# FFN in two phases over a DRAM copy of the gated features, and grid tokens laid out in blocks of 8 columns

## Chip, cores, metric

One core of a Trainium2 chip runs the whole program. The metric is the device time of one execution in microseconds (us), the median over the runs of a kernel. TensorE is called PE here, VectorE DVE, ScalarE ACT, GpSimd POOL; SyncE (SP) issues nearly all DMAs, and its queue is worked off in order.

## What is computed

Two layers with shared structure run over 128 context tokens and 1024 latent tokens (a grid of 16 rows by 64 columns). In each layer:

```
h = rms_norm(x) * (1 + sc_m) + sh_m
q, k, v of three head groups = split(h @ w_in)      # 6 neighbourhood heads, 4 MLA heads, 6 GQA heads
# neighbourhood head, latent token at (r, c): keys of 8 rows (clipped) x 16 columns (clipped) + 128 cached context keys,
#   col_start = clip(c - 8, 0, 48), row_start = clip(r - 4, 0, 8); bias rpb[row offset, column offset]
# MLA and GQA heads: all 1024 latent keys + 128 context keys
x = x + gt_m * rms_norm(concat(o_na, o_mla, o_gqa) @ w_out)
h = rms_norm(x) * (1 + sc_f) + sh_f
u = h @ w_up                                        # 1024 -> 2 x 2816
u = u[t-1] * conv_w[0] + u[t] * conv_w[1] + u[t+1] * conv_w[2] + conv_b     # along the tokens, t in row order of the grid
x = x + gt_f * rms_norm((silu(gate) * val) @ w_down)                        # 2816 -> 1024
```

## The kernel before

Tokens stand in 9 tiles of 128: tile 0 is the context, tiles 1 to 8 are the latent tokens, two grid rows each. Products are computed to float32 accuracy from pairs of float32r operands (a rounded part "hi" and a rest "lo"): hi*hi, hi*lo and lo*hi, so each product is three matmuls. `load_w` brings 128x1024 float32 weights into `wraw` (2 buffers), ACT casts them to "hi", and POOL or DVE subtracts to get "lo" (`split`). Instructions are put in order by a scheduler when the program is built; each engine then works off its own list in order.

A layer runs through these stages:

- **phase_a**: projections of h. The first product of layer 1 (values, weights `w0`) follows the FFN of layer 0 directly, and takes h tile by tile as the norm generators (`norm_tiles`, `h_group`) deliver it.
- **phase_b**: attention, head by head: 4 MLA and 6 GQA heads (`Task.dense`), then 6 neighbourhood heads (`Task.na`). A head is 8 tiles of 128 queries and one of context. A step scores one tile (`SA`), lets DVE add bias and mask and take the maximum (L829), ACT take the exponential, POOL normalise it (L708); three steps later PE transposes the probabilities (L719), ACT and DVE evacuate them as hi and lo (L200, L201), and PE multiplies by V (`pv_items`, L737). With two grid rows in a tile, the 8-row window of a query tile reaches over 4 tiles of keys in the tiles at the edge and 5 inside, plus the context tile: 640 or 768 columns. `load_bias` brings bias and mask as one `bint` tile and four `bedge` tiles, 17 pieces a head with their memsets.
- **phase_c**: output projection, norm, residual.
- **phase_d**: the FFN, in one loop over 22 features `f` of 128. For each it does the up products of the gate (`pg`, 3 PSUM banks of 384 tokens) and of the value (`pv_`, 3 banks): 72 matmuls each (L1025). `conv` gives ACT the centre tap and DVE the two shifted taps (`shifted`, L1037); ACT does SiLU; `gate` multiplies on POOL (L1059) and splits the result into `g`. Every second feature, `down` multiplies the two waiting `g` with their `w_down` rows for all 9 token tiles into `aux` (2 banks), 6 matmuls a bank (L1072), and DVE adds each bank into `Y` in SBUF (L1077). Beside it run the generators `extra` (`ada_dve`, L306): DVE's share of the modulation vectors, in layer 0 also those of layer 1.
- **The end of the FFN** (`last`): the last two features' products are done tile by tile; then `norm_tiles` reads `Y`, normalises, adds the residual, stores x, and in layer 0 makes h of layer 1. Tiles go in `PAIRS`.

## Time and profile before

| | |
|---|---|
| median of 3 runs | 3474.81 us (3470.6 to 3475.94) |
| the profiled execution | 3465.22 us |
| its span, first to last instruction | 3463.4 us |
| granted PE clock, mean | 0.982 of 2.4 GHz |
| busy: PE, DVE, ACT, POOL | 3266.7, 2263.4, 1486.0, 1073.9 us (94, 65, 43, 31%) |
| DMA | 339.33 MB, mean 98 GB/s |

The stages in us from the span's start: attention of layer 0 from about 365 to 758, its FFN from 889.0 to 1754.2, the values' product of layer 1 to 1832.7, attention of layer 1 from about 2060 to 2480, its FFN from 2602.9 to the end. PE is the engine to look at first: what counts is where it waits, and for whom, stage by stage, and not its share of the whole.

### The profile page before, as it was taken

How to read it: one execution, taken by the hardware profiler on the slowest of the kernel's cores; microseconds unless marked ns; L12 is line 12 of the kernel's file. 1: busy time of each engine (PE TensorE's matmuls, PEld its weight loads, DVE VectorE, ACT ScalarE, POOL GpSimd, SP SyncE). 2: the span in 40 equal slices, each digit the busy share in tenths (PEclk: the TensorE clock that was granted, in tenths of full speed). 3: DMA queues.
4: the chain of work that ended last, by engine and by line, in shares of the span. 5: the costliest groups of instructions: out<-in, count | busy, mean ns of one | idle time of the engine just before them, and what ended most of it. 6: DMA issues, size and time to landing. Idle time of an engine off the chain costs nothing. (4 is left out here: it accounts for less than half of the span.)

```text
span 3463.4 us, 50333 instructions
## 1 busy us (share of the span) xinstructions
PE 3266.7 (94%) x18380; PEld 2936.7 (85%) x18380; DVE 2263.4 (65%) x4955; ACT 1486.0 (43%) x3085; POOL 1073.9 (31%) x1062
## 2 busy tenths in 40 slices
PE   8989999999999999999988899999989999999996
PEld 4868888877889889899967799888779999999995
DVE  5796788886756755655497728888877433334437
ACT  4321788884422222222264228888753222222222
POOL 2121445541322222222242314455312223222223
PEclk9999999999999999999999899999999999999998
DMA  6467421453222222221144563115523111111113
GB/s 236 137 186 225 135 67 45 108 149 128 97 80 85 86 61 67 85 74 61 43 143 125 148 187 102 52 44 138 172 94 96 49 43 49 43 43 43 37 38 115
DMA packets 193415, 339.33 MB, mean 98 GB/s; under 512 B 18448, under 2 KB 107920, under 8 KB 193168
## 3 DMA queue, kind: packets, MB, share of 16 engines
q1 hardware_dynamic: 191872, 334.93, 32.4%
q8 instruction: 145, 2.38, 0.3%
q10 hardware_dynamic: 1296, 1.19, 0.1%
q14 instruction: 102, 0.84, 0.1%
HBM read 260.61 MB, written 75.43 MB: 97 GB/s over the span
## 5 line engine op out<-in xcount | busy, mean ns | idle before, releaser
L1025 PE MATMUL mm<-hhi,wu 128*128 128x384 f32 x4224 | 873.7, 336 | 2.4 <-POOL wu L195 1.5
L1025 PEld LDWEIGHTS mm<-hhi,wu 128*128 128x128 f32 x4224 | 746.8, 188 | 7.1 <-POOL wu L195 2.1
L1037 DVE SCALAR_TENSOR_TENSOR acc<-mm,conv,acc 128x127 f32<-128x127 f32 (+2 forms) x704 | 314.6, 509 | 335.3 <-ACT acc L1042 335.1
L1072 PE MATMUL aux<-wd,g 128*128 128x512 f32 x2160 | 501.5, 391 | 16.3 <-DVE Y L1077 11.3
L1025 PE MATMUL mm<-hlo,wu 128*128 128x384 f32 x2112 | 497.5, 335 | 0.0
L1072 PEld LDWEIGHTS aux<-wd,g 128*128 128x128 f32 x2160 | 405.3, 188 | 101.8 <-DVE Y L1077 13.4
L1025 PEld LDWEIGHTS mm<-hlo,wu 128*128 128x128 f32 x2112 | 379.4, 188 | 0.8 <-DVE hlo L151 0.4
L195 POOL TENSOR_TENSOR wu<-wraw,wu 128x1024 fp32r<-128x1024 f32 x90 | 218.8, 2433 | 466.5 <-ACT wu L192 433.7
L737 PE MATMUL O<-PT,V 128*128 128x256 f32 (+1 forms) x2080 | 349.3, 296 | 6.5 <-DVE Y L744 3.9
L1077 DVE TENSOR_TENSOR Y<-Y,aux 128x512 f32<-128x512 f32 x324 | 220.8, 686 | 182.3 <-PE aux L1072 181.9
L708 POOL TENSOR_SCALAR P<-P,rs 128x1152 f32<-128x1152 f32 (+3 forms) x288 | 291.2, 1012 | 151.3 <-DVE rs L707 120.7
L719 PE MATMUL T<-ident,P 128*128 128x128 f32 x1856 | 299.1, 277 | 16.5 <-DVE PT L201 11.5
L689 PE MATMUL SA<-k,q 128*128 128x512 f32 (+5 forms) x1224 | 301.0, 366 | 8.5 <-ACT ko L611 4.0
L195 POOL TENSOR_TENSOR wd<-wraw,wd 128x1024 fp32r<-128x1024 f32 x46 | 111.2, 2417 | 631.1 <-ACT wd L192 631.1
L201 DVE TENSOR_TENSOR PT<-T,PT 128x512 fp32r<-128x512 f32 (+1 forms) x448 | 290.2, 656 | 25.1 <-ACT PT L200 19.2
L737 PEld LDWEIGHTS O<-PT,V 128*128 128x128 f32 x2080 | 279.1, 190 | 21.5 <-DVE Y L744 10.0
L192 ACT CAST wd<-wraw 128x1024 fp32r<-128x1024 f32 x50 | 52.4, 1050 | 524.5 <-PE aux L1072 401.0
L200 ACT CAST PT<-T 128x512 fp32r<-128x512 f32 (+1 forms) x448 | 247.7, 568 | 57.2 <-PE T L719 44.2
L719 PEld LDWEIGHTS T<-ident,P 128*128 128x128 f32 x1856 | 213.9, 141 | 57.1 <-DVE PT L201 16.1
L306 DVE SCALAR_TENSOR_TENSOR aacc<-wadv,sc,aacc 128x512 f32<-128x512 f32 x280 | 218.7, 814 | 46.5 <-DMA wadv<-w_ada 45.5
L689 PEld LDWEIGHTS SA<-k,q 128*128 128x128 f32 (+1 forms) x1224 | 199.1, 192 | 33.6 <-ACT P L699 6.7
L192 ACT CAST wu<-wraw 128x1024 fp32r<-128x1024 f32 x94 | 98.7, 1052 | 260.4 <-PE mm L1025 260.1
(222 smaller groups left out, 5232.8 us busy)
## 6 DMA issues: line engine op xcount, KB each, us to landing
wraw<-w_up SPq DMA_DIRECT2D x88, 512.0 KB, 3.5
wadv<-w_ada SPq DMA_DIRECT2D x160, 256.0 KB, 2.7
wraw<-w_down SPq DMA_DIRECT2D x44, 512.0 KB, 3.5
k<-KT SPq DMA_DIRECT2D x64, 320.0 KB, 6.2
q<-QT SPq DMA_DIRECT2D x48, 288.0 KB, 5.2
XD<-xt SPq DMA_DIRECT2D x27, 512.0 KB, 2.6
xt<-XD SPq DMA_DIRECT2D x27, 512.0 KB, 4.2
wraw<-w_in SPq DMA_DIRECT2D x24, 512.0 KB, 3.7
```

The lines of the kernel that those rows point to most:

```text
L195: (lo_eng or pool).tensor_tensor(out=lo, in0=raw, in1=hi.bitcast(F32), op=ALU.subtract)
L200: act.copy(hi, src)
L201: dve.tensor_tensor(out=lo, in0=src, in1=hi.bitcast(F32), op=ALU.subtract)
L306: dve.scalar_tensor_tensor(out=accs[i], in0=w, scalar=sc[:, k, i:i + 1], in1=accs[i], op0=ALU.mult, op1=ALU.add)
L689: pe.matmul(out, q[0:rows, qc:qc + 128], kview(k[0:rows]), start=(i == 0), stop=(i == len(passes) - 1))
L708: pool.tensor_scalar(out=P[:, :n], in0=P[:, :n], scalar1=rs, scalar2=1.0, op0=ALU.mult, op1=ALU.mult)
L719: pe.transpose(tp[:, j * 128:(j + 1) * 128], p, ident)
L737: pe.matmul(op[0][:, :n], V[:, vt, :], PT[e][:, sl, :n], start=(i == 0 and e == 0), stop=(i == last and e == 1))
L1025: pe.matmul(pts[c][:, :CN], a[:, k, :], h_[:, k, c * CN:(c + 1) * CN], start=(k == 0 and a is whi and h_ is hhi), stop=(k == KC - 1 and a ...
L1037: dve.scalar_tensor_tensor(out=d, in0=pts[c][:, lo_ - c * CN:hi_ - c * CN], scalar=cw[:, wi:wi + 1], in1=d, op0=ALU.mult, op1=ALU.add)
L1072: pe.matmul(pt, g[:, ts], d[:, 0, js], start=(n == 0), stop=(n == tot - 1))
L1077: dve.tensor_tensor(out=Y[:, t, js], in0=Y[:, t, js], in1=pt, op=ALU.add)
```

## The change

Two things are changed, in both layers.

**Grid tokens by blocks of 8 columns.** The host reorders the latent tokens, so that a tile of 128 holds all 16 rows of 8 columns. The 16-column window of a query tile then reaches over 3 tiles of keys (2 at the two edges) and the context tile: 512 or 384 columns. The row window is done by the mask alone. One bias tile a head comes in one DMA (`b_na`). Probabilities of a tile go through one transposing step instead of one and a half; a pair of query tiles shares slots of `PT`, and keys that only one of them sees are multiplied by V in 128 columns. The convolution runs along grid rows, so neighbours at a block's edge now stand in another tile: `shifted` takes 7 of 8 columns inside the blocks and further small pieces for the edges, 8 instructions for each direction instead of 4.

**FFN in two phases.** `phase_u` does up products, convolution and gate for all 22 features and stores the gated values, unsplit, in DRAM (`GT`, 576 KB a feature). `Down` then goes over groups of three token tiles. A group keeps 6 PSUM banks open over all 22 features; for each it loads the `w_down` rows again (512 KB) and the group's slice of `GT` (192 KB), splits both, and does 18 matmuls. `Y`, its adds and the two-bank `aux` stage are gone. A tile is normalised from PSUM when its group is done (`tile_done`), the tiles of a group one after the other, with the last 2 features of a group (4 at the very end) done tile by tile. Splits of even steps put the weights' lo on POOL and the gated values' on DVE, odd steps the other way round. Loads run 3 features ahead. In the last layer each tile of y is stored in two halves.

```diff
+            b = bp.tile([128, 1280], F32, name="bias", bufs=2)
+            nc.sync.dma_start(out=b, in_=I["b_na"][l, h])
+            return [b[:, 512:896]] + [b[:, 0:512]] * 6 + [b[:, 896:1280]]
...
-            for i, (vt, sl) in enumerate(slots):
+            for i, (vt, sl, c0, c1) in enumerate(slots):
                 if not op:
                     op.append(bps.tile([128, 256], F32, name="O", bufs=1))
                 for e in range(2):
-                    pe.matmul(op[0][:, :n], V[:, vt, :], PT[e][:, sl, :n],
+                    pe.matmul(op[0][:, c0:c1], V[:, vt, :], PT[e][:, sl, c0:c1],
...
             def na(self, hd, pair, a):
                 i = 2 * pair + a
+                lo, hi = max(i - 1, 0), min(i + 2, 8)
+                n = self.n = (hi - lo + 1) * 128
                 qc = 128 + i * 128
+                k0 = 2 + lo
                 m = small("mx")
                 s = bank2()
                 self.P = new_p()
                 self.pieces, self.mneg, self.sign = [(self.P[:, :n], 0)], m[:, 0:1], -1.0
                 def sc_a():
+                    scores(s[:, 0:256], hd.passes, qc,
                            lambda k: k.rearrange("p (b n) -> p b n", n=128)[:, 1:k0 + 1:k0 - 1, :])
+                    scores(s[:, 256:n], hd.passes, qc,
+                           lambda k: k[:, (k0 + 1) * 128:(2 + hi) * 128])
+                    dve.tensor_tensor_reduce(out=self.P[:, :n], in0=s[:, 0:n],
                                              in1=hd.bias[i][:, :n], op0=ALU.add, op1=ALU.min, scale=-1.0,
                                              scalar=3.0e38, accum_out=m[:, 0:1])
                 self.sc = [sc_a]
+                own = [0, 2, 3, 1] if a == 0 and pair else list(range(hi - lo + 1))
                 qs = slice(a * 128, (a + 1) * 128)
+                def tr():
+                    if a == 0:
                         hd.PT[pair] = new_pt()
+                    transpose_p([self.block(b) for b in own],
+                                [o[:, 0:len(own), qs] for o in hd.PT[pair]])
+                self.tr = [tr]
+                b0 = 2 + 2 * pair
+                slots = [(1, 0, 0, 256)]
+                if pair > 0:
+                    slots.append((b0 - 1, 3, 0, 128))
+                if pair < 3:
+                    slots.append((b0 + 2, 3, 128, 256))
+                slots += [(b0, 1, 0, 256), (b0 + 1, 2, 0, 256)]
+                self.pv = (lambda: pv_items(hd.V, hd.PT[pair], slots, 256, hd.hg,
+                                            128 + pair * 256)) if a == 1 else None
                 return self
...
+            fr = slice(0, 7) if sh == 1 else slice(1, 8)
+            to = slice(1, 8) if sh == 1 else slice(0, 7)
+            fe, te = (7, 0) if sh == 1 else (0, 7)
+            b0, nb, o = (0, 2, 128) if c == 0 else (3 * c - 1, 3, 0)
+            if c == 0:
+                f0 = 0 if sh == 1 else 1
+                add(acc[:, f0 + sh:f0 + sh + 127], pts[0][:, f0:f0 + 127])
+            src = pts[c][:, o:o + nb * 128].rearrange("p (g i) -> p g i", i=8)
+            dst = acc[:, 128:NT].rearrange("p (g i) -> p g i", i=8)
+            add(dst[:, b0 * 16:(b0 + nb) * 16, to], src[:, :, fr])
+            if sh == 1:
+                n = min(nb, 7 - b0) * 16
+                add(dst[:, (b0 + 1) * 16:(b0 + 1) * 16 + n, te], src[:, 0:n, fe])
+                if n < nb * 16:
+                    add(dst[:, 1:16, te], src[:, n:n + 15, fe])
+            else:
+                k = 1 if b0 == 0 else 0
+                add(dst[:, (b0 + k - 1) * 16:(b0 + nb - 1) * 16, te], src[:, k * 16:nb * 16, fe])
+                if k:
+                    add(dst[:, 112:127, te], src[:, 1:16, fe])
...
+        def gate(ag, av):
+            pool.tensor_tensor(out=av, in0=ag, in1=av, op=ALU.mult)
+            nc.sync.dma_start(out=GT[l][f], in_=av)
+
+        def along():
+            for _ in range(3):
+                advance(extra)
...
             else:
                 up_mm(wg, pg, range(NCH))
+            ag = conv(pg, f, 0)
+            act.activation(out=ag, in_=ag, func=AF.Silu)
+            along()
+            if f > 0:
                 wv = load_up(f + NFF)
                 pv_ = [mm() for _ in range(NCH)]
                 up_mm(wv, pv_, range(NCH))
+            av = conv(pv_, f + NFF, 1)
+            gate(ag, av)
+            along()
...
+    DOWN = ((0, 1, 2), (3, 4, 5), (6, 7, 8))
+    AHEAD = 3
+    class Down:
+        def __init__(self, l, wp, gp):
+            self.l, self.wp, self.gp = l, wp, gp
+            self.seq = [(g, f) for g in range(len(DOWN)) for f in range(NFF)]
+            self.parts = {}
+        def load(self, i):
+            if i >= len(self.seq) or i in self.parts:
+                return
+            g, f = self.seq[i]
+            e, o = (dve, pool) if i % 2 else (pool, dve)
+            wd = load_w(self.wp, I["w_down"][self.l, f], ("wd", "wu")[i // 2 % 2], 2, e)
+            n = 128 * len(DOWN[g])
+            raw = self.gp.tile([128, CN], F32, name="graw", bufs=2)[:, :n]
+            nc.sync.dma_start(out=raw, in_=GT[self.l][f][:, DOWN[g][0] * 128:DOWN[g][0] * 128 + n])
+            gs = [self.gp.tile([128, CN], F32R, name=f"g{j}", bufs=4)[:, :n] for j in range(2)]
+            split(raw, *gs, lo_eng=o)
+            self.parts[i] = gs, wd
+        def products(self, i, t, pts, js):
+            g, f = self.seq[i]
+            (ghi, glo), (dhi, dlo) = self.parts[i]
+            ts = slice((t - DOWN[g][0]) * 128, (t - DOWN[g][0] + 1) * 128)
+            for n, (a, d) in enumerate(((ghi, dhi), (ghi, dlo), (glo, dhi))):
+                for j in js:
+                    pe.matmul(pts[j], a[:, ts], d[:, 0, j * 512:(j + 1) * 512], start=(f == 0 and n == 0),
+                              stop=(f == NFF - 1 and n == 2))
+        def run(self, tile_done, step, before_tail, tail_last):
+            for g, tiles in enumerate(DOWN):
+                end = g == len(DOWN) - 1
+                tail = tail_last if end else 2
+                pts = {t: [mm(), mm()] for t in tiles}
+                i0 = g * NFF
+                for f in range(NFF - tail):
+                    self.load(i0 + f + AHEAD)
+                    for t in tiles:
+                        self.products(i0 + f, t, pts[t], (0, 1))
+                    step()
+                for f in range(NFF - tail, NFF):
+                    self.load(i0 + f)
+                self.load(i0 + NFF)
+                if end:
+                    before_tail()
+                for t in tiles:
+                    for j in (0, 1):
+                        for f in range(NFF - tail, NFF):
+                            self.products(i0 + f, t, pts[t], (j,))
+                    tile_done(t, pts[t])
+                self.load(i0 + NFF + 1)
+                self.load(i0 + NFF + 2)
...
+        def tile_done(t, banks):
+            xt = load_x(ep, XD[2 * l], t, "xt", 4)
+            wt = ep.tile([128, D], F32, name="wt", bufs=4)
+            A, B = (zn.Am, zn.mods[:, 0]) if zn is not None else (None, None)
+            gens.append(norm_tiles(ep, (t,), [banks], [junk], [wt], [xt], G, xo, A, B, H, xs, GROUPS, (dve, dve)))
...
+        down.run(tile_done, lambda: advance(gens), lambda: more_w0((0, 1)), 4 if zn is None else 2)
+        more_w0((2, 3))
```

What an engine works off, and in which order, is decided when the program is built. Three places matter for what follows; the numbers behind names are buffers.

The first is SP's list in the middle of the FFN of layer 1. Before, loads of the up weights (`w_up`, two a feature) and of the down weights (`w_down`, one a feature) follow each other:

```order
L343 DMA wraw_32215<-w_down 128x1024
L343 DMA wraw_32221<-w_up 128x1024
L343 DMA wraw_32459<-w_up 128x1024
L343 DMA wraw_32557<-w_down 128x1024
L343 DMA wraw_32563<-w_up 128x1024
L343 DMA wraw_32657<-w_up 128x1024
L343 DMA wraw_32755<-w_down 128x1024
```

In the change the stores of the gated values stand among the loads of the up weights. Here `GT16` and `GT17` are features 6 and 7 of layer 1, and the loads ahead of each store are those of the feature two further on (8 ahead of the store of 6, 9 ahead of 7):

```order
L348 DMA wraw_29603<-w_up 128x1024
L348 DMA wraw_29705<-w_up 128x1024
L1054 DMA GT16_116<-acc1_29376 128x1152
L348 DMA wraw_29808<-w_up 128x1024
L348 DMA wraw_29910<-w_up 128x1024
L1054 DMA GT17_117<-acc1_29581 128x1152
L348 DMA wraw_30013<-w_up 128x1024
L348 DMA wraw_30115<-w_up 128x1024
```

The down weights' loads have left this stretch, and a store, which waits for POOL's product of its feature, has none of the next feature's loads behind it.

The second is SP's list in the down phase, a stretch that did not exist before (the loads of `w_down` then stood among those of `w_up`, as above). This is group 0 of layer 0, features 12 to 15, the slice of gated values (`graw`) and the weights (`wraw`) of each:

```order
L1109 DMA graw_15984<-GT012_100 128x384
L348 DMA wraw_15978<-w_down 128x1024
L1109 DMA graw_16014<-GT013_101 128x384
L348 DMA wraw_16008<-w_down 128x1024
L1109 DMA graw_16044<-GT014_102 128x384
L348 DMA wraw_16038<-w_down 128x1024
L1109 DMA graw_16074<-GT015_103 128x384
L348 DMA wraw_16068<-w_down 128x1024
```

Before, a load of `w_down` stood between every two of `w_up`; now each feature of each group has two loads, alternately, and each waits for the split that frees its buffer two features back: `wraw` for POOL's in even features and for DVE's in odd ones, `graw` the other way round.

The third is PE's list in the last neighbourhood head of layer 0 (`k0`, `k1` are hi and lo of the keys, `SA` scores, `T` transposed probabilities, `O` the product with V). Before, two inner tiles:

```order
L689 MATMUL SA_9449<-k0_9130,q0_9138 128x256
L689 MATMUL SA_9449<-k1_9133,q0_9138 128x256
L689 MATMUL SA_9449<-k0_9130,q0_9138 128x512
L689 MATMUL SA_9449<-k1_9133,q0_9138 128x512
L719 MATMUL T_9464<-ident_63,P_9354 128x128 x4
L737 MATMUL O_9471<-PT1_9400,V_8818 128x256
L737 MATMUL O_9471<-PT0_9399,V_8818 128x256
L737 MATMUL O_9471<-PT1_9400,V_8818 128x256
L689 MATMUL SA_9486<-k0_9130,q0_9138 128x256
L689 MATMUL SA_9486<-k1_9133,q0_9138 128x256
L689 MATMUL SA_9486<-k0_9130,q0_9138 128x512
L689 MATMUL SA_9486<-k1_9133,q0_9138 128x512
```

Now, an inner tile and the product of an inner pair:

```order
L679 MATMUL SA_8662<-k0_8394,q0_8402 128x256
L679 MATMUL SA_8662<-k1_8397,q0_8402 128x256
L679 MATMUL SA_8662<-k0_8394,q0_8402 128x256
L727 MATMUL O_8618<-PT0_8553,V_8146 128x256
L679 MATMUL SA_8662<-k1_8397,q0_8402 128x256
L727 MATMUL O_8618<-PT1_8554,V_8146 128x256
L727 MATMUL O_8618<-PT0_8553,V_8146 128x128
L727 MATMUL O_8618<-PT1_8554,V_8146 128x128
L727 MATMUL O_8618<-PT0_8553,V_8146 128x128
L727 MATMUL O_8618<-PT1_8554,V_8146 128x128
L727 MATMUL O_8618<-PT0_8553,V_8146 128x256
L727 MATMUL O_8618<-PT1_8554,V_8146 128x256
```

The second score piece went from 512 to 256 columns, the transposes of a tile from five or six to four, and the product of an inner pair from 14 matmuls of 256 columns to 10, of which four have 128.

## Rows read from the trace of the kernel before

**Rows 1.** Windows by stage: length, busy us of each engine (instructions), clock, DMA, GB/s.

```profile
889.00:1832.70 943.70, 907.97 (x4762) 837.64 (x4760) 593.84 (x1045) 265.69 (x401) 254.60 (x130) 0.99 0.26 81
1754.20:1832.70 78.50, 65.27 (x282) 48.69 (x280) 64.68 (x155) 48.95 (x106) 30.58 (x30) 0.91 0.46 148
2602.90:3463.40 860.50, 827.55 (x4391) 776.27 (x4389) 401.68 (x746) 216.59 (x300) 237.33 (x109) 0.99 0.17 56
3438.80:3463.40 24.60, 0.22 (x1) 0.00 (x0) 20.76 (x53) 3.61 (x10) 8.30 (x6) 0.57 0.55 199
682.00:701.00 19.00, 18.33 (x137) 16.48 (x137) 17.73 (x46) 16.62 (x39) 9.31 (x23) 1.00 0.82 214
```

**Rows 2.** PE's waits in the FFN of layer 0: us, times, longest.

```profile
PE aux L1072 <- DVE Y L1077: 11.3, 5, 3.4
```

**Rows 3.** Timeline of PE, up products: start, us, what.

```profile
3254.81 1.20 PE L1025 MATMUL mm<-hhi,wu 128*128 128x384 f32 x6
...
3256.37 1.20 PE L1025 MATMUL mm<-hhi,wu 128*128 128x384 f32 x6
```

**Rows 4.** Timeline of PE, output projection, two banks in turn.

```profile
827.89 1.07 PE L989 MATMUL mm<-wx,hhi 128*128 128x512 f32 x4
...
829.25 1.07 PE L989 MATMUL mm<-wx,hhi 128*128 128x512 f32 x4
```

**Rows 5.** Groups by shape, six neighbourhood heads, 644 to 757 us: busy, mean ns.

```profile
L201 DVE TENSOR_TENSOR PT<-T,PT 128x512 fp32r<-128x512 f32 x51 | 34.7, 683 | 5.1 <-ACT PT L200 4.3 <-issue 0.2
L829 DVE CUSTOM_DVE_ANT_0 P<-SA,bint 128x768 f32<-128x768 f32 x24 | 22.8, 950 | 2.2 <-POOL P L708 0.7 <-PE SA L689 0.6 <-PE T L719 0.5
L829 DVE CUSTOM_DVE_ANT_0 P<-SA,bedge 128x640 f32<-128x640 f32 x24 | 19.5, 814 | 1.2 <-PE SA L689 1.0 <-issue 0.2
```

**Rows 6.** Timeline of PE in a neighbourhood head.

```profile
689.87 1.45 PE L737 MATMUL O<-PT,V 128*128 128x256 f32 x10
691.16 0.96 PE L689 MATMUL SA<-k,q 128*128 128x256 f32 x4
...
697.14 0.42 PE L737 MATMUL O<-PT,V 128*128 128x128 f32 x2
697.40 0.52 PE L719 MATMUL SB<-ident,P 128*128 128x128 f32 x3
```

**Rows 7.** Groups by shape, FFN of layer 0, 889 to 1725 us.

```profile
L306 DVE SCALAR_TENSOR_TENSOR aacc<-wadv,sc,aacc 128x512 f32<-128x512 f32 x168 | 131.5, 819 | 24.7 <-DMA wadv<-w_ada 23.9
L1077 DVE TENSOR_TENSOR Y<-Y,aux 128x512 f32<-128x512 f32 x162 | 110.3, 685 | 82.0 <-PE aux L1072 81.6
L1037 DVE SCALAR_TENSOR_TENSOR acc<-mm,conv,acc 128x127 f32<-128x127 f32 x88 | 30.2, 343 | 82.0 <-ACT acc L1042 81.9
```

**Rows 8.** The page's costliest groups, whole span.

```profile
L1037 DVE SCALAR_TENSOR_TENSOR acc<-mm,conv,acc 128x127 f32<-128x127 f32 (+2 forms) x704 | 314.6, 509 | 335.3 <-ACT acc L1042 335.1
```

**Rows 9.** The chain that ended last, its end: start, us, what.

```profile
3457.32 0.08 DVE nw_u L118
...
3459.13 0.66 DVEq L1371
```

**Rows 10.** Tile wraw, FFN of layer 1: ns min/median/max, first and last start.

```profile
L192 ACT CAST wu<-wraw x42: 1048/1052/1066, 2629.8 to 3382.2; 128x1024 fp32r<-128x1024 f32 x42
L195 POOL TENSOR_TENSOR wu<-wraw,wu x42: 2390/2404/3204, 2631.0 to 3383.4; 128x1024 fp32r<-128x1024 f32 x42
...
DMA to landing us min/median/max: 3.3/3.5/4.5
```

**Rows 11.** Timelines of POOL and DVE in the output projection of layer 0.

```profile
770.36 2.87 POOL L195 TENSOR_TENSOR wd<-wraw,wd 128x1024 fp32r<-128x1024 f32 x1 [5.58 <-ACT wd L192]
...
771.26 3.05 DVE L195 TENSOR_TENSOR hlo<-Y,hhi 128x1024 fp32r<-128x1024 f32 x1 [0.29 <-ACT hhi L192]
```

**Rows 12.** Timeline of PE after the FFN of layer 0, and a window there.

```profile
1763.18 0.79 PE L370 MATMUL mm<-wd,hhi 128*128 128x512 f32 x1 [3.08 <-DVE wd L195]
...
1763.10:1767.00 3.90, 3.82 (x9) 3.01 (x10) 3.73 (x15) 2.10 (x3) 0.00 (x0) 0.53 0.00 0
```

More of the change, by code (lines that the diff above doesn't have):

```diff
@@ L68, in tile_kernel @@
     VM = [dram.tile([4, 128, NTT + 1, 128], F32, name=f"VM{l}") for l in range(L)]
+    GT = [[dram.tile([128, NT], F32, name=f"GT{l}{f}") for f in range(NFF)] for l in range(L)]
     psum = None
@@ L1126, in phase_d @@
-        ready.append((g, wd))
-        for c in range(NCH + 1):
-            if c < NCH:
-                up_mm(wv, pv_, (c,))
-                centre(av, pv_, f + NFF, c)
-                shifted(av, pv_, f + NFF, c, -1)
-            if c:
-                shifted(av, pv_, f + NFF, c - 1, 1)
-                gate(ag, av, g, slice((c - 1) * CN, c * CN), dve)
-        for t in range(NTT):
-            last(t, lambda j: down(ready, t, j, first, mm))
+    DOWN = ((0, 1, 2), (3, 4, 5), (6, 7, 8))
+    AHEAD = 3
@@ L1249, in pend_done @@
                 ex.append(ada_dve(l + 1, zn, p, (1, 0, 2, 3, 4), 512))
[L1250 to L1265 removed]
+            return p, [chain(*ex)]
@@ new lines, in tile_kernel, with more_w0 @@
+        phase_u(l, z, H, wp, pend, pend_done)
+        down.load(0)
+        down.load(1)
+        down.load(2)
+        dst.close()
+        xo = XD[2 * l + 1] if l + 1 < L else O["y"]
+        est, ep = right("ep")
+        junk = [ep.tile([128, D // 2], BF16, name=f"junk{j}") for j in range(2)]
+        gens, xs, owner = [], {}, {}
+        w0 = [], []
+        def more_w0(ii):
+            if zn is not None:
+                for i in ii:
+                    for a, b in zip(w0, load_w(wp, I["w_in"][l + 1, :, 2 * i:2 * i + 2, G_V[0]:G_V[0] + G_V[1]],
+                                               ("wu", "wd")[i // 2], 2, dve if i % 2 else pool)):
+                        a += [b[:, 0], b[:, 1]]
```

193 lines of the change are left out of this document (43 added, 150 removed).

## The prediction

> **Bound.** I read the page first: PE is busy 94% of the span, so the question is where its other 6% lie, and which of its work the change takes away. Windows by stage answer the first. From the first up product of the FFN of layer 0 to the end of the values' product of layer 1, 943.7 us pass with PE busy for 908.0; in the last 78.5 us of that, 13 us are idle and the granted clock is 0.91. From the start of the FFN of layer 1 to the end, 860.5 us pass, and in the last 24.6 of them PE does nothing [rows 1]. The list of PE's waits inside the FFN of layer 0 names DVE's add into `Y`: 11.3 us [rows 2]. In the timeline PE's pace is seen where it does not wait: nine up matmuls start every 1.56 us (3254.81 to 3256.37) [rows 3], and six matmuls of 512 columns on two banks in turn every 1.36 us (827.89 to 829.25) [rows 4]. In a neighbourhood head (19 us) PE is busy for 18.3, DVE for 17.7, ACT for 16.6 and the DMA engines for 82% [rows 1]: four resources near their limit, so such a head gets shorter only if all four get less, and here all four do.
>
> **Neighbourhood heads.** DVE: the score step costs 950 ns for 768 columns and 814 for 640 [rows 5], so 1.06 ns a column; 512 columns should take 0.68, 384 0.54. A head has four tiles of each kind before (7.06 us) and six of 512 with two of 384 after (5.15). The lo evacuations are ten of 512 and two of 256 columns before (10 x 0.683 + 2 x 0.41 = 7.65, 0.41 by the same slope) and six of 512 with two of 384 after (5.2) [rows 5]. DVE loses 4.4 us of 17.7; at today's density (17.7 in 19) a head takes 14.3. PE: scores, transposes and products with V are 124 matmuls before (4 x 17 inner, 4 x 14 edge) and 98 after (scores 32, transposes 30, V 36), with 5 for the context tile either way. The 128-column products that are new save nothing each: two of them take 0.26 us (697.14 to 697.40), ten of 256 take 1.29 (689.87 to 691.16) [rows 6], 0.13 each in both. By the count alone 18.3 becomes 18.3 x 103/129 = 14.6; the dropped 512-column pieces make it less. DMA: keys, queries and V stay (1280, 576 and 640 KB), bias falls from 1344 to 640 KB, so 82% of 19 us x 3136/3840 = 12.7 us. But bias stands behind V in SP's list, V waits until the head before last has left it, so I take 15 rather than 14.3: 4.0 us a head, 12 heads, -48. Bounds: 14.3 gives -56; 17.3, if latencies between the shorter steps show, gives -20.
>
> **Layer 0.** In its FFN and on the way into layer 1 matmuls neither come nor go. Up: 352 groups of nine, 549.1 us. Down: 198 groups of six, 269.3. Values' product: 216 matmuls, 49.0. Some 184 transposes at 0.13, as the short products of [rows 6]: 24. That is 891 us of the 943.7, so 52 are waits and slow clock [rows 1]. Gone are the waits for `Y`. Most of those behind the FFN go too: six of nine tiles are normalised and transposed while a later group multiplies, and two of four `w0` pieces come before the last products. What stays or comes new, 20 us in all: waits for the gate vectors (4), PSUM at the changes of group (2), the last `w0` pieces (5), the last tiles' h (4), DVE late (5). So -32. DVE per feature in the up phase: 16 shifted adds at 509 ns [rows 8], 8 us; 131.5 us of modulation over 22 features, 6 us; and 110.3 us of `Y`, 5 us [rows 7]. The `Y` adds go, and 16 more shifted adds come at no more than 343 ns, 5.5 us [rows 7]. So some 20 us a feature stay, but the period shrinks from 39 (865 over 22) to 25.0 us. That cover is thin: a bank has 12.5 us from its last product until PE wants it again, and an add can find eight modulation steps (8 x 0.82 = 6.6 us, some waiting for their DMA) ahead of it. If it fails by 2 us in 15 features, 30 us are lost; bounds -42 and -5. Two edits I cost at nothing: the larger number of small adds in layer 1 (no modulation there after the first features), and the stores of `GT`, since in SP's list the loads for the feature after next stand ahead of each store.
>
> **Layer 1.** By the same prices 549.1 + 269.3 + 2 = 820 of 860.5. Of the 24.6 us behind the last product [rows 1] about 8 stay: 4.3 from the last DVE work at 3459.13 to the end of the span, 1.8 for one tile's Newton steps and residual (from 3457.32) [rows 9], and 2 for its squares and gains (an estimate, as long). With 4 for the start and the group changes 832 remain: -28, bounds -33 and -15.
>
> **Loads.** In the down phase this is the part that could cost. PE uses a feature in 3 x 1.36 = 4.08 us, two in 8.16. Each `wraw` buffer serves every second feature. Its round in an even feature is 3.5 us from issue to landing, 1.05 for ACT, 2.40 for POOL [rows 10] and about 0.25 for hand-overs: 7.2, just under 8.16. With the longest landing in that row (4.5) it is 8.2, and with the longest POOL step (3.20) as well 9.0. Now 192 KB of gated values land beside each 512 KB, at 704 KB in 4.08 us, or 177 GB/s; windows of this trace show up to 214 [rows 1], so bandwidth suffices, and it is the round that counts. I take 8.35, nearer to the longest landing than to the median, since two transfers now overlap: 0.1 us a feature over 132 features, +13; bounds 0 and +55 (9.0).
>
> **Sum.** -48 - 32 - 28 + 13 = -95 against the profiled execution's 3465.2: 3370. The median of the runs stands 9.6 higher, so 3474.8 - 95 = 3380.
>
> **Rivals.** *The loads pace the down phase.* POOL's and DVE's subtractions meet there all the time, and where they met before, one of DVE's took 3.05 us (771.26 to 774.31), ending 1.1 after POOL's 2.87 had ended, and POOL's was longer than the median of [rows 10] [rows 11]. If such a step of 1.1 us regularly stands ahead of POOL's in the round, it is 9.1 us with landings of 4.3, 0.47 a feature: +62 instead of +13, 3429. Against it: four slots of weights, 12 us ahead, even out single delays. The Trainium skill, page "SBUF — State Buffer", section "Who interferes with whom", says that a DVE instruction with two SBUF inputs and a GpSimd instruction that reads SBUF exclude each other for the whole instruction; by that rule the sum would be this rival's 3429 instead of 3380, and the row at 771.26 agrees with it.
>
> *Neighbourhood heads hardly shrink*, because loads still gate them: the DMA share of 82% is for it, the smaller bias against. At 18 us a head -12 instead of -48: 3416.
>
> *Slower: PE falls to half its clock in the down phase.* After a wait of 3.08 us the granted clock was 0.53 from 1763.1 to 1767, and nine matmuls of 512 columns took 3.90 us, 0.43 each [rows 12]. A feature then takes 18 x 0.43 = 7.7 us instead of 4.08. If the loads fall behind so far that PE waits 2 or 3 us at a time, each feature at that clock loses 3.6; the gain of 108 that stands without the loads is used up when 30 of 132 run so, and 60 give +108: about 3583. For it: nothing covers a late load once the four slots are empty. Against it: waits of tenths of a microsecond are what the round predicts. The Trainium skill, page "TensorE: Matmul & The Clock Gate", section "HAM oscillation — how this bites in real kernels", describes a kernel in which waiting for the next slice put PE back to the low clock at every step; by that rule this rival is right as soon as waits get long, which the trace shows at 1763.
>
> **Numbers.** Forecast 0.56 (its own range 3340 to 3400), loads 0.23, heads 0.12, slower 0.09. The range 3335 to 3450 leaves out the last and the far ends of the others. A measurement tells about 0.2% (7 us) from no change; slower is the last rival, 0.09, the same 0.03, from the worst of the loads' case, faster 0.88.
>
> **Signs.** Right: neighbourhood heads 15 us apart; PE near 100% busy in the up phase with nine matmuls every 1.56 us; no wait for `Y`; under 10 us behind the last matmul. In the down phase PE's waits name DVE or POOL lo steps of `wd` and `wu` for some 13 us in all. Wrong: those waits sum to 50 or more, the granted clock falls below 0.95 there, up products wait for shifted adds in layer 0, or the heads stay over 17 us.

## The result, and the profile after

The changed kernel takes 3373.15 us (median of 4 runs, 3369.34 to 3376.69), the kernel before 3475.38 beside it: ratio 0.9706, interval 0.9691 to 0.9722. The forecast was 3380. The spans of the two profiled executions differ by 90.4 us (3463.4 to 3373.0), the medians by 102.2: the profiled execution of before lay 10 us under its median, that of the change (3374.83) 1.7 over. The working went by the profiled one, -95; stage by stage it is measured against -90.4.

Lines of the changed kernel: score step L818, evacuations of transposed probabilities L205 (ACT) and L206 (DVE), product with V L727 and its add L734, output projection L968, shifted adds L1015, up L1003, down L1120, splits of weights and gated values L197 (hi) and L200 (lo), the norm's Newton steps L116 and L120, its product with the gains `wt` L166, transposes and evacuation of h (`ht`) L148 and L152.

Windows by stage, columns as in [rows 1]: layer 0's up phase, its down phase, the values' product of layer 1 behind them, all three together; then for layer 1 up, down, both to the end, and the piece behind the last matmul.

```profile
876.10:1442.50 566.40, 563.50 (x3281) 560.46 (x3280) 423.04 (x963) 158.72 (x224) 174.79 (x74) 1.00 0.36 114
1442.50:1731.70 289.20, 280.16 (x1238) 229.38 (x1237) 132.59 (x251) 134.66 (x219) 124.64 (x76) 0.99 0.59 189
1731.70:1784.80 53.10, 52.20 (x239) 41.81 (x239) 28.31 (x80) 24.26 (x47) 9.83 (x10) 1.00 0.44 137
876.10:1784.80 908.70, 895.86 (x4755) 831.65 (x4754) 583.94 (x1293) 317.64 (x488) 309.26 (x160) 1.00 0.44 139
2535.10:3092.70 557.60, 554.65 (x3200) 551.95 (x3199) 252.99 (x768) 158.32 (x224) 170.01 (x74) 1.00 0.23 78
3092.70:3365.40 272.70, 270.07 (x1189) 222.56 (x1187) 110.89 (x176) 107.29 (x162) 112.58 (x63) 1.00 0.60 195
2535.10:3373.00 837.90, 824.88 (x4387) 774.51 (x4385) 367.34 (x955) 266.31 (x387) 282.59 (x137) 1.00 0.36 116
3365.40:3373.00 7.60, 0.16 (x1) 0.00 (x0) 3.46 (x11) 0.69 (x2) 0.00 (x0) 0.76 0.30 112
```

Against [rows 1] layer 0 went from 943.7 to 908.7 us (-35.0), layer 1 from 860.5 to 837.9 (-22.6), and behind the last matmul 7.6 us stay of 24.6. The larger part of both gains lies behind the FFN: in layer 0 the values' product takes 53.1 us for 78.5 (-25.4) and the FFN itself 855.6 for 865.2 (-9.6), in layer 1 it is -17.0 behind the last matmul and -5.6 before it. Most tiles are now normalised while a later group multiplies. PE's waits in the two down phases (layer 0, then layer 1, all rows), and then ACT's two longest in layer 1 (us, times, longest):

```profile
PE aux L148 <- DVE ht L152: 5.8, 3, 4.0
PE mm L1120 <- DVE wt L166: 2.6, 2, 1.3
PE aux L148 <- ACT wt L188: 0.6, 1, 0.6
...
PE mm L1120 <- DVE wt L166: 2.6, 2, 1.3
...
ACT g L197 <- PE mm L1120: 82.4, 39, 5.8
ACT wu L197 <- DMA wraw<-w_down: 24.1, 15, 4.6
```

No wait of PE names a load or a lo step of weights. It is ACT that waits, longest for PE to give back a `g` buffer; it also waits 43 us for weights to land in layer 1 (24.1 for `wu`, 19.1 for `wd`), but none of this reaches PE: the loads run ahead of the products. Tile `wraw` in layer 1's down phase, as in [rows 10]:

```profile
L197 ACT CAST wd<-wraw x32: 1043/1052/1057, 3101.3 to 3349.1; 128x1024 fp32r<-128x1024 f32 x32
L200 POOL TENSOR_TENSOR wd<-wraw,wd x16: 2388/2402/2732, 3102.4 to 3346.2; 128x1024 fp32r<-128x1024 f32 x16
...
DMA to landing us min/median/max: 3.3/3.6/5.6
```

The score steps of the six neighbourhood heads by line, layer 0 (first and last start), and groups by shape there, against [rows 5]:

```profile
L818 DVE CUSTOM_DVE_ANT_0 P<-SA,bias x48: 540/677/692, 648.0 to 738.9; 128x512 f32<-128x512 f32 x36, 128x384 f32<-128x384 f32 x12
```

```profile
L727 PE MATMUL O<-PT,V 128*128 128x256 f32 x161 | 34.3, 311 | 5.4 <-ACT PT L205 4.7 <-DVE PT L206 0.5
...
L206 DVE TENSOR_TENSOR PT<-T,PT 128x512 fp32r<-128x512 f32 x38 | 25.3, 685 | 3.4 <-ACT PT L205 3.2
L818 DVE CUSTOM_DVE_ANT_0 P<-SA,bias 128x512 f32<-128x512 f32 x36 | 24.5, 682 | 2.3 <-PE SA L679 2.3
...
L727 PE MATMUL O<-PT,V 128*128 128x128 f32 x70 | 11.1, 264 | 1.2 <-DVE Y L734 1.2
```

The first and the last score step are 90.9 us apart, 112.6 before (the row of before is below). That is 53 steps at nine a head: 15.4 us a head for 19.1. In layer 1 it is 90.9 for 112.5. Behind the last step it goes the other way: the first up product starts 137.2 us after it (738.9 to 876.1), 132.2 before; in layer 1 137.0 for 132.1. The sum over the span: heads -43.3, what is behind them +9.9, the FFNs -35.0 and -22.6, +0.6 elsewhere.

### The profile page after: what moved, and what is told of

It reads as the page before. It is cut to its first block, busy times and chain, and to the rows that moved or that the text cites. A ratio compares the mean times of both kernels' runs of the same rounds, so it can differ in the third digit from the quotient of the medians.

```text
span 3373.0 us, 51130 instructions
## 1 busy us (share of the span) xinstructions
PE 3209.3 (95%) x18068; PEld 2895.7 (86%) x18068; DVE 2165.7 (64%) x5367; ACT 1546.9 (46%) x3209; POOL 1127.5 (33%) x962
## 4 chain that ended last, share of the span: by engine, by line
PE 71%; DVE 13%; ACT 7%; issue 4%; DMA 3%; POOL 1%; SPq 0%; ACTq 0%; DVEq 0%; POOLq 0%
PE mm L1003 32%; PE mm L1120 15%; PE O L727 5%; PE T L709 4%; PE mm L968 4%; PE SA L679 4%; ACT P L689 3%; PE mm L591 2%; DVE PT L206 2%; ACT PT L205 2%; PE mm L375 1%; PE mm L376 1%; PE mm L374 1%; DVE nw_t L116 1%; PE SB L679 1%
## 5 line engine op out<-in xcount | busy, mean ns | idle before, releaser
L1003 PE MATMUL mm<-hhi,wu 128*128 128x384 f32 x4224 | 863.4, 335 | 3.1 <-POOL wu L200 2.2
L1003 PEld LDWEIGHTS mm<-hhi,wu 128*128 128x128 f32 x4224 | 742.7, 188 | 4.3 <-POOL wu L200 2.8
L1015 DVE SCALAR_TENSOR_TENSOR acc<-mm,conv,acc 128x336 f32<-128x336 f32 (+6 forms) x1408 | 412.5, 375 | 314.8 <-ACT acc L1040 314.5
L200 POOL TENSOR_TENSOR wu<-wraw,wu 128x1024 fp32r<-128x1024 f32 x123 | 302.2, 2458 | 690.3 <-ACT wu L197 690.2
L1003 PE MATMUL mm<-hlo,wu 128*128 128x384 f32 x2112 | 490.9, 334 | 0.0
L197 ACT CAST wu<-wraw 128x1024 fp32r<-128x1024 f32 x158 | 165.7, 1051 | 593.6 <-issue 369.6
L1003 PEld LDWEIGHTS mm<-hlo,wu 128*128 128x128 f32 x2112 | 377.1, 188 | 0.6 <-DVE hlo L153 0.4
L727 PE MATMUL O<-PT,V 128*128 128x256 f32 (+1 forms) x1936 | 334.4, 299 | 22.6 <-ACT PT L205 10.5
L311 DVE SCALAR_TENSOR_TENSOR aacc<-wadv,sc,aacc 128x512 f32<-128x512 f32 x280 | 261.2, 976 | 63.5 <-DMA wadv<-w_ada 63.3
L206 DVE TENSOR_TENSOR PT<-T,PT 128x512 fp32r<-128x512 f32 (+1 forms) x448 | 284.4, 650 | 23.9 <-ACT PT L205 18.9
L727 PEld LDWEIGHTS O<-PT,V 128*128 128x128 f32 x1936 | 263.1, 192 | 40.2 <-ACT PT L205 16.7
L679 PE MATMUL SA<-k,q 128*128 128x256 f32 (+5 forms) x1224 | 283.8, 353 | 9.2 <-ACT ko L616 4.0
L1120 PE MATMUL mm<-wd,g 128*128 128x512 f32 x1224 | 288.1, 392 | 2.6 <-DVE wt L166 2.6
L1120 PEld LDWEIGHTS mm<-wd,g 128*128 128x128 f32 x1224 | 230.2, 189 | 51.4 <-DVE wt L166 3.5
L1120 PE MATMUL mm<-wu,g 128*128 128x512 f32 x1152 | 270.7, 391 | 2.6 <-DVE wt L166 2.6
L205 ACT CAST PT<-T 128x512 fp32r<-128x512 f32 (+1 forms) x448 | 241.9, 563 | 58.3 <-PE T L709 46.3
L1120 PEld LDWEIGHTS mm<-wu,g 128*128 128x128 f32 x1152 | 216.4, 188 | 48.2 <-DVE wt L166 3.5
L702 DVE TENSOR_REDUCE mx<-SA 128x1 f32<-128x896 f32 (+1 forms) x192 | 182.4, 950 | 36.6 <-PE SA L679 36.6
```

Source lines behind the costliest of these rows:

```text
L200: (lo_eng or pool).tensor_tensor(out=lo, in0=raw, in1=hi.bitcast(F32), op=ALU.subtract)
L205: act.copy(hi, src)
L206: dve.tensor_tensor(out=lo, in0=src, in1=hi.bitcast(F32), op=ALU.subtract)
L311: dve.scalar_tensor_tensor(out=accs[i], in0=w, scalar=sc[:, k, i:i + 1], in1=accs[i], op0=ALU.mult, op1=ALU.add)
L679: pe.matmul(out, q[0:rows, qc:qc + 128], kview(k[0:rows]), start=(i == 0), stop=(i == len(passes) - 1))
L702: dve.tensor_reduce(out=out, in_=src, op=ALU.max, axis=AX.X, negate=True)
```

## Experiments

Medians are compared with the 3373.15 of the change; the kernel before, run beside them, stayed at 3473.2 to 3473.7.

**The two parts apart.** Grid rows with their heads, bias and shifted adds as before; the FFN as in the change.

```diff
-            return [b[:, 512:896]] + [b[:, 0:512]] * 6 + [b[:, 896:1280]]
...
+            for i in range(8):
+                if 2 <= i < 6:
+                    bt[i] = bint
...
-            add(dst[:, b0 * 16:(b0 + nb) * 16, to], src[:, :, fr])
...
+                d = acc[:, lo_ + sh:hi_ + sh]
```

> The two parts of the change taken apart: grid tokens in rows of the grid again (heads with 640 and 768 columns, 17 bias pieces, four shifted adds a direction), the FFN in two phases as in the change; nothing is left out. Theory A (the terms of the forecast add up): the two phases alone keep the FFN's gain as the traces show it, 35.0 us in layer 0 and 22.6 in layer 1, and the heads go back from 15.4 to 19.1 us, 43 us in all; 3373 + 43 = 3416 us. Theory B (the blocks cost something in the FFN, where their small shifted adds come twice as often and hold the PSUM banks longer): the up phases get shorter by 5 us or more each (566.4 and 557.6 us in the change) and the total stays under 3406. The 5.0 us by which the change's stage from the last score step to the first up product grew (132.2 to 137.2) go back to 132 if the blocks caused them.

3401.47 us (ratio to before 0.9791, 0.9778 to 0.9805): the two phases give 72 us, the blocks 28. Its heads by line, with the row of before ahead of it in a fence of its own:

```profile
L829 DVE CUSTOM_DVE_ANT_0 P<-SA,bedge x24: 802/814/825, 644.2 to 756.8; 128x640 f32<-128x640 f32 x24
```

```profile
L834 DVE CUSTOM_DVE_ANT_0 P<-SA,bedge x24: 804/815/826, 647.2 to 759.8; 128x640 f32<-128x640 f32 x24
```

The heads are those of before, 112.6 us, so the blocks earn their 43 us there. They lose part of it: behind the heads the first up product comes 131.7 us after the last step here (759.8 to 891.5), so the +5 a layer belongs to the blocks. In the up phases, theory B's place, they cost only 1.3 and 2.0 us:

```profile
891.50:1456.60 565.10, 563.50 (x3281) 560.43 (x3280) 376.15 (x619) 158.55 (x225) 176.96 (x74) 1.00 0.35 114
...
2563.40:3119.00 555.60, 554.34 (x3199) 551.89 (x3199) 206.30 (x424) 158.27 (x224) 169.09 (x74) 1.00 0.23 78
```

So theory B had the total and the wrong place. Theory A's sum, 3416, is 15 us too high: 11 of them lie behind the heads (131.7 and 131.8 us, for 137.2 and 137.0 in the change), 3 in the up phases.

**All subtractions of the down phase on DVE.**

```diff
-            e, o = (dve, pool) if i % 2 else (pool, dve)
+            e = o = dve
```

> The changed kernel with every subtraction of the down phase on DVE (weights and gated values, 1.22 and 0.55 us a feature) and none on POOL; nothing is left out. In the change, one-column steps of DVE that take 0.22 us elsewhere take 2.3 us at 1533.8 and 1543.0 while POOL subtracts. Theory A (DVE and POOL hold each other up, and that is what makes DVE late at the changes of group): such steps fall to about 0.2 us, the two waits of 1.3 us for wt in each layer go, the 5.8 us of waits for ht in layer 0 shrink; layer 0's down phase falls from 289.2 to about 282, layer 1's from 272.7 to 270; total 3363 to 3366. Theory B (DVE is late since it has much to do there): with 2.4 us more of its own for each second feature it is later still; the waits stay or grow, total 3373 to 3380. The load round alone (5.9 us in place of 7.3, against PE's 8.16 for two features) gives nothing by either.

3363.09 us (0.9683, 0.9670 to 0.9696), 10 less than the change. What theory A is about, in the changed kernel, DVE's timeline and then POOL's at the first change of group in layer 0:

```profile
1533.76 2.36 DVE L116 SCALAR_TENSOR_TENSOR nw_t<-nw_u,nw_v 128x1 f32<-128x1 f32 x1
1536.04 0.68 DVE L166 TENSOR_TENSOR wt<-mm,G 128x512 f32<-128x512 f32 x1
```

```profile
1533.36 2.74 POOL L200 TENSOR_TENSOR wd<-wraw,wd 128x1024 fp32r<-128x1024 f32 x1 [7.78 <-ACT wd L197]
```

A step on one column lasts 2.36 us and ends (1536.12) when POOL's subtraction ends (1536.10); behind it stands the `wt` that gives PE its bank back. The Trainium skill, page "SBUF — State Buffer", section "Who interferes with whom", has it so: a DVE instruction with two inputs in SBUF, as this step is, and a GpSimd instruction that reads SBUF contend for ports that only one of them can hold. With POOL out, the group of these steps falls from a mean of 435 ns (change, first) to 214:

```profile
L116 DVE SCALAR_TENSOR_TENSOR nw_t<-nw_u,nw_v 128x1 f32<-128x1 f32 x39 | 16.6, 435 | 0.5
```

```profile
L116 DVE SCALAR_TENSOR_TENSOR nw_t<-nw_u,nw_v 128x1 f32<-128x1 f32 x39 | 7.6, 214 | 0.2
```

```profile
1437.70:1718.10 280.40, 276.60 (x1238) 226.84 (x1237) 164.10 (x313) 134.04 (x219) 16.60 (x14) 1.00 0.61 195
3080.20:3349.80 269.60, 269.60 (x1190) 222.70 (x1188) 145.29 (x238) 107.23 (x162) 2.69 (x1) 1.00 0.61 197
```

The down phases fall from 289.2 and 272.7 to 280.4 and 269.6 us (the windows above), and no wait of PE for DVE's `wt` is left, though DVE has more to do (110.9 to 145.3 us in layer 1). In layer 0 PE's waits for `ht` fall from 5.8 to 1.4 us. This is theory A.

**Four groups.** More loads for the same products.

```diff
-    DOWN = ((0, 1, 2), (3, 4, 5), (6, 7, 8))
+    DOWN = ((0, 1), (2, 3), (4, 5), (6, 7, 8))
```

> The changed kernel with four groups of token tiles (2, 2, 2 and 3) in place of three, so 88 loads of weights a layer in place of 66; nothing is left out. PE then needs 2.72 us a feature in the groups of two, 5.44 for two, and the round of a weight buffer in even features is 7.3 us (landing 3.6, ACT 1.05, POOL 2.4, hand-overs 0.25). Theory A (the round sets the pace as soon as it is longer than PE's time, and costs only the difference): 66 features at 3.65 and 22 at 4.08, 331 us in place of 269, +62 a layer; total about 3497 us. Theory B (PE also falls to its half clock in the waits): a feature of 12 products at 0.43 us takes 5.2, +160 a layer, total about 3695 and a granted clock near 0.5 there. Theory C (the loads run ahead and never pace): within 15 us of the change, 3373 to 3388.

3488.34 us (1.0046, 1.0033 to 1.0060), 15 us slower than the kernel before. Windows of the two down phases:

```profile
1439.70:1781.70 342.00, 296.21 (x1238) 226.11 (x1236) 172.77 (x272) 155.91 (x261) 159.71 (x97) 0.99 0.60 191
3146.60:3477.10 330.50, 286.60 (x1190) 221.07 (x1188) 149.25 (x198) 130.15 (x206) 153.30 (x85) 0.99 0.61 197
```

PE's longest waits in the second:

```profile
PE mm L1120 <- POOL wu L200: 21.1, 15, 1.9
PE mm L1120 <- POOL wd L200: 16.9, 12, 1.7
```

330.5 us where the round gave 331, and the waits name POOL's step. The last digit is luck: 331 was worked out with the change's landing of 3.6 us, and with this run's own median of 3.8 the round gives 337. So the round is right to about 2%; with three groups it is shorter than PE's time. With waits of up to 1.9 us the mean granted clock was 0.99, so theory B fell; it dropped for short stretches only (0.92 from 3240 to 3260).

**Four groups, all subtractions on DVE.** Both diffs above together.

> The kernel with four groups of token tiles, with every subtraction of the down phase on DVE; nothing is left out. With four groups the down phases took 341.5 and 330.2 us, and PE's waits there named POOL's subtraction. Theory A (the round of a weight buffer sets the pace, and POOL's 2.4 us is a part of it): the round falls from 7.5 (landing 3.8, ACT 1.05, POOL 2.4, hand-overs 0.25) to 6.3 us, 3.16 a feature against PE's 2.72; 66 x 3.16 + 22 x 4.08 = 298 us in layer 1, about 31 less in each layer, total about 3422. Theory B (the DMA engines set the pace at 195 to 227 GB/s): 325 to 332 us stay, total 3475 to 3488.

3415.73 us (0.9836, 0.9820 to 0.9851), down phases:

```profile
1442.80:1745.30 302.50, 290.17 (x1238) 223.52 (x1236) 189.26 (x356) 154.43 (x261) 17.14 (x13) 0.99 0.66 216
3109.20:3406.60 297.40, 285.57 (x1190) 217.07 (x1188) 169.65 (x282) 129.90 (x206) 5.24 (x1) 1.00 0.68 219
```

297.4 against the 298 of theory A; with this run's own landing (median 3.6, not 3.8) the round gives 292, again within 2%. POOL's 2.4 us was part of the round, and the DMA engines could bring 219 GB/s, more than the 197 with POOL. What PE waits for in layer 1 (11 us in all) is no longer a weight buffer in the main:

```profile
PE mm L1120 <- ACT g L197: 8.3, 14, 2.0
```

That is ACT's cast of the gated values, which stands behind that of the weights. Which of the two buffers sets the pace here is not shown.

**Products with V later, in two banks.** `tag` is `O` and `SB` in turn, pair by pair.

```diff
-                    op.append(bps.tile([128, 256], F32, name="O", bufs=1))
+                    op.append(bps.tile([128, 256], F32, name=tag, bufs=1))
...
+            pvq.extend(held)
+            held.clear()
             if old and old.pv:
-                pvq.append(old.pv())
+                (held if old.late else pvq).append(old.pv())
```

> The changed kernel with the products of probabilities and V in the neighbourhood heads one step later, and in two PSUM banks in turn in place of one; nothing is left out. In the change, PE waits 9 us in the six heads of layer 0 (90.9 us), 4.7 of them for ACT's evacuation of PT and 1.2 for DVE's add of the product before. Theory A (what keeps a head at 15.4 us where PE's work is 13.9 is the latency between short steps): those waits go, a head takes 14.6, 12 heads give 10 us, total about 3363. Theory B (loads of V and bias gate the heads, as the forecast argued for 15 in place of 14.3): no change, 3371 to 3375. Theory C: the products that are now later stand behind other score steps and make new waits; 3373 to 3380.

3359.68 us (0.9673, 0.9659 to 0.9686), 13 less, but not where theory A put it: the score steps stay 91.2 and 89.6 us apart. The gain lies behind the last head. PE there, in the change:

```profile
742.98 1.41 PE L727 MATMUL O<-PT,V 128*128 128x256 f32 x10
...
748.47 2.92 PE L727 MATMUL O<-PT,V 128*128 128x256 f32 x10 [3.54 <-DVE Y L734]
...
757.10 1.22 PE L968 MATMUL mm<-wu,hhi 128*128 128x512 f32 x2 [2.04 <-ACT hhi L197]
```

and DVE:

```profile
745.33 2.54 DVE L200 TENSOR_TENSOR wu<-wraw,wu 128x1024 fp32r<-128x1024 f32 x1 [1.20 <-ACT wu L197]
747.90 0.42 DVE L734 TENSOR_TENSOR Y<-O,otmp 64x256 f32<-64x256 f32 x1
748.35 1.29 DVE L206 TENSOR_TENSOR PT<-T,PT 128x512 fp32r<-128x512 f32 x2
```

DVE's subtraction for the first weights of the output projection stands ahead of the add of a product and of three evacuations of transposed probabilities. PE waits 3.54 us, and ten matmuls then take 2.92 us, 1.41 at 742.98. The granted clock is 0.50 from there into the projection:

```profile
748.40:760.00 11.60, 8.83 (x28) 7.00 (x29) 6.87 (x9) 7.21 (x10) 2.36 (x1) 0.50 0.49 167
```

The projection starts 18.2 us after the last score step (757.1 less 738.9). Before, this subtraction stood behind the last evacuation, and it was 10.7 (767.49 less 756.8):

```profile
763.19 0.42 DVE L201 TENSOR_TENSOR PT<-SB,PT 128x256 fp32r<-128x256 f32 x1
764.09 1.77 DVE L195 TENSOR_TENSOR wu<-wraw,wu 128x1024 fp32r<-128x1024 f32 x1 [0.47 <-ACT wu L192]
...
767.49 2.93 PE L989 MATMUL mm<-wu,hhi 128*128 128x512 f32 x6 [2.82 <-ACT hhi L192]
```

With the later products:

```profile
743.20 1.16 PE L727 MATMUL O<-PT,V 128*128 128x128 f32 x8
744.20 1.49 PE L727 MATMUL SB<-PT,V 128*128 128x256 f32 x8
750.48 2.08 PE L973 MATMUL mm<-wu,hhi 128*128 128x512 f32 x4 [4.80 <-ACT hhi L197]
```

The projection starts 10.5 us after the last step (740.0), as before the change. Its own start is at half clock there and in the kernel before as well (0.51 from 750.4 to 755, 0.54 from 767.5 to 774); what the change added is the slow stretch ahead of it.

**Two banks alone.** The same `tag`, without `held`.

> The changed kernel with the neighbourhood products with V in two PSUM banks in turn, and no step later than in the change; nothing is left out. Behind the last head of layer 0 the changed kernel waits 3.5 us for DVE's add of the product before, ten matmuls then take 2.9 us in place of 1.4, and the output projection starts 17.7 us after the last score step; with later products and two banks it started 10.0 us after it. Theory A (the one bank does it): the projection starts about 10 us after the last score step here too, total 3360 to 3364. Theory B (the later step does it, since products then no longer stand ahead of transposes): the distance stays near 17 us, total 3370 to 3375.

3371.96 us (0.9710, 0.9695 to 0.9725); the projection starts 17.8 us after the last step (739.8 to 757.55). Theory B: the two banks alone do not do it, the later step with them does. A later step in one bank was not run.

**Bias once a layer.**

```diff
-                hd.bias = load_bias(h)
+                bias0 = bias0 if h else load_bias(h)
+                hd.bias = bias0
```

> The changed kernel with the bias tile of head 0 loaded once a layer and used for all six neighbourhood heads, so five loads of 640 KB a layer are left out (and the heads 1 to 5 use a bias that is not theirs). Theory A (loads do not gate the heads: in the run with later products PE's waits for them sum to 1.0 us in the six heads of layer 0, and that kernel's heads stayed at 15.5 us): heads stay within 0.2 us of 15.4, total 3369 to 3376. Theory B (bias behind V in SP's list gates them, as the forecast argued for 15 in place of 14.3): a head falls to 14.6 or less, total 3363 or less.

3368.30 us (0.9697, 0.9680 to 0.9714); score steps 91.4 and 91.2 us apart, not less than in the change. So bias loads do not hold the change's heads (theory A). Loads of keys, queries and V were not left out, but no wait of PE, DVE or ACT in the heads names a load. The 5 us by which the run is shorter lie behind the heads: the first up product comes 133.7 and 133.8 us after the last step, for 137.2 and 137.0.

This run also happens to move DVE's subtraction (to 746.16, ahead of one evacuation), and its projection starts 14.7 us after the last step. So the start follows the place of that subtraction in DVE's list: ahead of three evacuations 18.2 and 17.8 us (the change, two banks alone), ahead of one 14.7, behind the last 10.7, 10.9 and 10.5 (before, rows with two phases, later products).

**Both edits.** `e = o = dve` and the later products.

> The changed kernel with both edits that made it faster: the down phase's subtractions all on DVE, and the neighbourhood products with V one step later in two banks; nothing is left out. Theory A (the two act in different stages and add up: 10.1 and 13.5 us): 3350 us. Theory B (they share a cause, or the gain of one was only the start of the program, which differed by up to 4 us between the profiled executions): 3355 to 3362.

3348.18 us (0.9640, 0.9625 to 0.9654), 25 less than the change, for 10 and 13 apart: they add up (theory A).

**Three on what holds a head**, each on the kernel with both edits: a longer lag, and the two that leave work out.

```diff
-        hist, pvq, held, lag = [], [], [], 3
+        hist, pvq, held, lag = [], [], [], 4
```

> The kernel with both edits, and a probability tile transposed four steps after its scores in place of three; nothing is left out. In that kernel six neighbourhood heads pass in 90.7 us (15.4 a head; PE is busy 82.8 of them, DVE 78.5, ACT 78.1), and 2.0 us of PE's waits in them are for POOL's normalisation. Theory A (a head is held by the latency from score to transpose): it falls to 14.9 or less, 12 heads give 6 us or more, total 3338 to 3342. Theory B (PE, DVE and ACT hand short pieces of like sums to each other in order; an earlier start of one piece helps none): heads stay within 0.2 us, and the emptying at the end of attention takes one step more, 1.7 us a layer; total 3348 to 3352.

3352.21 us (0.9651, 0.9636 to 0.9666): score steps 90.9 and 93.5 us apart, 89.5 and 89.4 (15.2 a head) without it. Not shorter, so theory A fell. Theory B's total came, its heads within 0.2 us did not: they are 0.2 and 0.7 us a head longer, and in layer 1 DVE waits 2.3 us for loads of bias.

```diff
+            if hg < 6:
+                act.copy(Y[ro:ro + 64, hg // 2, t0:t0 + n], op[0][0:64, :n])
+                yield
+                return
```

> The kernel with both edits; in the neighbourhood heads, DVE's add of the two halves of a product with V is left out (ACT copies one half to the output), so the output lacks the lo half of V there. DVE loses 4 adds of 0.42 and one of 0.28 us a head, 2.0 of its 13.3. Theory A (DVE holds the head): six heads pass in 79 to 83 us in place of 90.7. Theory B (PE holds it): within 2 us of 90.7. Theory C (ACT, DVE and PE hold it in turn): a part of DVE's 2.0 us a head shows, 84 to 88 us.

One run, 3347.59 us; 87.9 and 89.5 us. Taking 12 us in all from DVE gives 1.6 us in layer 0 and nothing in layer 1. But now DVE waits for bias, in layer 0 of the kernel with both edits, then here:

```profile
DVE P L818 <- DMA bias<-b_na: 0.2, 1, 0.2
```

```profile
DVE P L823 <- DMA bias<-b_na: 3.9, 2, 2.5
```

In layer 1 it is 4.7 us, for 0.4. So the loads come next as soon as DVE has less to do, and the run does not tell what a head would take without them.

```diff
-                for e in range(2):
+                es = (0,) if tag == "SB" or t0 > 0 and n == 256 and len(slots) < 9 else (0, 1)
+                for e in es:
```

> The kernel with both edits; in the neighbourhood heads the products with the lo half of the probabilities are left out for the latent tokens, 18 of 103 matmuls a head, 2.3 us of PE's 14.1 (the output lacks that part). Theory A (PE holds the head): six heads pass in 78 to 82 us in place of 90.7, down to the 78.5 of DVE. Theory B (DVE or ACT holds it): within 2 us of 90.7. Theory C (held in turn): 83 to 88 us.

One run, 3351.86 us; 95.3 and 92.7 us, so longer with 18 matmuls fewer a head. In layer 0 one stretch of it ran at half clock (0.50 from 709 to 718); in layer 1, over a window 1 us wider than the steps, the clock was full:

```profile
2291.30:2385.20 93.90, 79.07 (x560) 66.08 (x558) 78.66 (x244) 77.09 (x202) 36.57 (x57) 1.00 0.64 164
```

So neither less work of PE or of DVE alone, nor a longer lag makes a head shorter by more than 0.3 us, and where DVE has less work it waits for bias loads. What sets a head's 15 us is left open; less work of DVE together with one bias load was not run.

## Why the prediction was right, step by step

**Neighbourhood heads, -48: right in kind, -43.3.** DVE's step costs came out as worked out (512 columns 0.68, 384 0.55 us), and 128-column products cost what wide ones do: eight of them start from 743.20 to 744.20 in the run with later products, 0.125 us each, and ten of 256 columns from 742.98 to 744.22 in the change, 0.124. A head takes 15.4 us, not 15. The reason given for the 0.7 above DVE's 14.3, loads of V and bias, is not borne out: the run that loads bias once is no shorter in the heads, and no wait there names a load of V. What holds the heads in its place is open, so that 15 came close to 15.4 is in part luck. The rival of 18 us a head fell with the measured 15.4.

**Missing: what is behind the last head, +9.9.** No step of the forecast looked at how attention empties into the output projection. There the blocks moved DVE's subtraction for weights ahead of the last products. The run with rows shows that it comes with the blocks, the run with later products gives it back.

**Layer 0, -32: -35.0, with the loads in it.** Up: 549.1 for 3168 up products, 113 short matmuls at 0.13 (14.7) and 2.6 of waits make 566.4, as measured. Nine up matmuls start every 1.56 us (1002.44 to 1004.00) and none waits for shifted adds, so the thin cover held and the 5 us for a late DVE in the up phase were not spent. The down phase took them: 289.2 is 269.3 for products, 6.2 for 48 transposes and 9.0 of waits, and 5 more, of which about 3 are the clock (an estimate from 3.2 us at 0.56 and 5.8 us at 0.72). At the first change of group it fell behind the longest of the waits, to 0.56 from 1557.4 to 1560.6; six products there are followed by the next after 2.46 us, 1.36 at the full clock [rows 4]:

```profile
1557.37 1.11 PE L148 MATMUL aux<-ident,wt 128*128 128x128 f32 x4 [3.95 <-DVE ht L152]
1558.13 2.59 PE L1120 MATMUL mm<-wu,g 128*128 128x512 f32 x6
```

At the second it was 0.72 from 1659.4 to 1665.2, behind waits of 0.60 and 1.61 us. The waits of 2.6 and 5.8 us for `wt` and `ht` were in the main DVE held by POOL, which I had looked for in the loads: with POOL out, 3.8 us of idle time stay of these 9.0 and 1 of the 5, at a clock of 1.00.

**Layer 1, -28: -22.6, mis-sized.** The end was right (7.6 us behind the last matmul, 8 said). Mis-sized are the terms beside the products, 2 and 4 us for the rest and for the start and the group changes: the two phases took 11.9 us more than the 549.1 and 269.3 of the products. Of these, 4.2 are 32 short matmuls among the up products (3200 less 3168, at 0.13), as layer 0's sum had counted them, 2.7 are waits in the up phase, 2.6 waits for `wt`, and 2.4 are not assigned.

**Loads, +13: wrong, nothing.** The failed step is "I take 8.35, nearer to the longest landing than to the median, since two transfers now overlap". The landing's median went from 3.5 to 3.6 us only, so the round is 3.6 + 1.05 + 2.40 + 0.25 = 7.3, under PE's 8.16, and landings of 5.6 were covered by the slots. The rival that the loads pace had the right mechanism, POOL and DVE excluding each other, at a place where it costs nothing; four groups show what it costs where the round is longer than PE's time. The rival of half the clock needed waits of 2 or 3 us for loads; none came. What the Trainium skill, page "TensorE: Matmul & The Clock Gate", section "HAM oscillation — how this bites in real kernels", tells of waiting for the next slice appeared where PE waited for DVE instead: behind the last head, where a wait of 3.54 us was followed by matmuls at a clock of 0.50, and at the first change of group in layer 0.

**Sum.** Heads 4.7 short, 9.9 unforeseen, FFN and loads together -57.6 where -47 was said, 0.6 elsewhere: 4.6 short of -95. Errors of 14.6 and 10.6 us nearly cancel, so the nearness of 3373 to 3380 is in part luck. By the medians the gain was 102.2. Of the signs, heads 15 us apart, nine up matmuls every 1.56 us, no wait for `Y` and under 10 us at the end came; the 13 us of waits for lo steps of `wd` and `wu` did not.

## What to carry to other kernels

Price a load that runs beside products by the round of its buffer against the time PE needs for as many pieces as there are buffers: here 7.3 against 8.16 cost nothing, and 7.3 against 5.44 cost 55 us a layer. When stages get shorter, look at their seams: what the next stage puts into the queue of an engine that the last steps still need. An engine that seems to have nothing on the path (POOL) can stand there through another that it holds up; moving its work to the busier DVE was worth 10 us.
